# Single-head attention steps, weights split two half tiles ahead, an opening in program order, and a last down product by column halves, in a two-layer hybrid decoder trunk

## The chip, the core and the metric

The kernel runs on one core of a Trainium2 chip. Its five engines run their own instruction streams in order: TensorE (PE, with its weight loads as PEld), VectorE (DVE), ScalarE (ACT), GpSimd (POOL) and SyncE (SP), which issues the large weight transfers. The metric is the device time in microseconds, the median of the runs; one execution is also profiled. Times in the profile count from the start of the profiled span.

## The reference

Two layers over 256 tokens of width 1024, batch 1, all float32:

```python
proj = x @ w_in[l]                        # q, k, v, conv (3 parts), memory queries, three gates
y_attn = diff_attention(rope(q), rope(k), v, lam, ...)     # 8 heads, two score maps per head
y_conv = short_gated_conv(cb, cc, cu, conv_w[l])
y_mem = memory_attention(qm, mem, w_mem_kv[l])             # 4 heads on 256 memory tokens
merged = sum of sigmoid(gate_i) * (y_i @ w_br_i)
x = layer_norm(ALPHA * x + merged @ w_out[l])
f = grouped_moe(x, ...)                   # 16 experts, the two best of one group of four per token
x = layer_norm(ALPHA * x + f)
```

## The kernel before

**Weights.** `plan` lists every weight tile of about 1 MB in the order of its use, and SP's queue fetches them in this order, `ahead` tiles in front of the use, into a ring of 19 buffers of 8 KB per partition (tag "L"). All other large tiles lie in the same ring. Outside the experts, a product in float32 accuracy is made of three fast ones: `pump` splits half a weight tile on ACT (`hl`, the rounded high part, L177) and DVE (the rest, L179), and `ws_block` multiplies high by high, high by low and low by high. The activations are split likewise (`th`/`tl` for the current input, L204 and L205). One *unit* is such a product with one half tile: 24 matmuls of 256 columns in `ws_block` (L215 to L218), or 12 of 512 columns in `mv_units` (L361). `use` hands out the next split half and calls `pump` only when none is ready. Expert weights are used whole and unsplit (`whole`).

**Order.** PE's instructions stand in program order (`manual_schedule`). DVE's and ACT's order is made by a scheduler, save in sections that name those engines too; each engine then runs its list strictly in order.

**Opening.** PE transposes the memory tokens (L290), the keys and values of memory follow (`mem_units`, eight units), then the input `x` is transposed. The tables of the rotary embedding (`sin`, `cos`, 25 small DVE operations and two on ACT) are written behind this in the program.

**Mixers.** `proj` is a generator that yields after every unit: `q` and `k` of a pair of heads (with the rotation on ACT and DVE, L472 to L477), `v`, memory queries, convolution. The loop in `mixers` takes six jobs, four pairs of heads and two pairs of memory heads, and lets `fill` run units between their parts: scores of both heads, 5200, the end of the job before, 5200, both transposes, 2600, the product with `v` (a unit counts 2600). Before the first pair, in layer 0 only, `columns` and `sums` turn small parameters into columns; `sums` has two exponentials (`lexp`) for lambda. Gates and branch products follow for four column blocks, then `w_out`.

**Experts.** `moe` routes the tokens, then runs eight pairs of experts: `project` (gate and up, L1061), `gated`, `hidden` (transposes, L1083), `down` (L1096), `combine` (L1110, into four accumulators). In the last pair the residual is rebuilt on DVE (`xt` from `xl` and `xh`, L1133, then gain and shift `gb`, L1146), the next layer's memory is transposed, and an overflow branch (L1156), not taken here, is passed after the last `down`. Then come `residual` (L314, with row sums), `moments`, `normalise`, and the next layer's `mem_units`.

Of the kernel before, what the change touches and what calls it, by code (L numbers as in the profile page):

```python
# [20 lines left out]
D = 1024  # L21
# [17 lines left out]
WARM = 5  # L39
FILL = 20700  # L40
NU = 5
APART = (5200, 5200, 2600)
# [11 lines left out]
def trunk(ctx: ExitStack, tc: tile.TileContext, x, mem, positions, w_in, lq1, lk1, lq2, lk2, subln, conv_w,  # L54
# [31 lines left out]
    def proj_tiles(w, p):  # L86

        return [([((slice(0, 4),), w[2 * p + i].rearrange("(p k) n -> p k n", p=128)[:, h * 4:h * 4 + 4, :])], (4, 512))
                for h in range(2) for i in range(2)]

    def down_tiles(w, p):
        return [([((slice(0, 2),), w[2 * p + i].rearrange("(p k) n -> p k n", p=128)[:, h * 2:h * 2 + 2, :])], (2, 1024))
                for h in range(2) for i in range(2)]
# [64 lines left out]
    def pump(n=1):  # L158

        while n > 0:  # L160
            if not halves:
                i = state["taken"]
                if i == len(plan):
                    return
# [28 lines left out]
    def use():  # L193
        if not ready:
            pump()
        return ready.pop(0)
# [85 lines left out]

    def transposed(src):
# [20 lines left out]

    def residual(xt, acc, st, t):

        sm = sb.tile([128, 2], F32, name="rsum", bufs=4)
        for c in range(2):
            added(xt, acc, sm, t, c)
        moments(xt, sm, st, t)  # L310
# [56 lines left out]

    mT = {0: transposed(mts.pop(0))}
# [15 lines left out]
    for name, quarter in (("sin", 0.0), ("cos", 0.25)):  # L384
# [20 lines left out]
        rope[name] = tab  # L405
    cosb = rope["cos"][:, None, :].to_broadcast([128, 2, S])
# [50 lines left out]
    def proj(l, xT, qk, vt, br, late2):  # L457
# [9 lines left out]
        for p in range(4):  # L467
# [11 lines left out]
            if p % 2 == 0:  # L479
# [8 lines left out]
        for j in range(2):  # L488
# [17 lines left out]
            split(ych[:, 2 * j:2 * j + 2, :], ycl[:, 2 * j:2 * j + 2, :], y)  # L506

# [12 lines left out]
    def attention(l, p, qk, vt, yT, values):  # L520

        q, k = qk.pop((p, "q")), qk.pop((p, "k"))
        probs = {}
        segs = ((0, 128), (128, 384))
        for h in range(2):
# [23 lines left out]
            nc.vector.tensor_scalar(st[:, 2, 1], st[:, 2, 1], par["nlam"][:, l:l + 1], None, op0=OP.mult)  # L549
# [5 lines left out]
            probs[h] = pr[0]  # L555
        yield
        aT = []
        for h in range(2):
            b = bank([128, 3, 128], "acc")
            for i in range(3):  # L560
                nc.tensor.transpose(b[:, i, :], probs[h][:, i * 128:(i + 1) * 128], ident)
            a = small([128, 3, 128], F32, "aT")
            nc.scalar.activation(a, b, AF.Copy)
            aT.append(a)
        yield
        values(p // 2)
        o = bank([128, 2, 2, 128], "acc")
        for h in range(2):
            c = (2 * p + h) * 128
            a = aT[h]  # L570
            mm(o[:, h, 0, :], a[:, 0, :], vt[:, 0, c:c + 128], start=True, stop=True)
            mm(o[:, h, 1, :], a[:, 1, :], vt[:, 0, c:c + 128], start=True, stop=False)
            mm(o[:, h, 1, :], a[:, 2, :], vt[:, 1, c:c + 128], start=False, stop=True)
        sq = small([128, 128], F32, "sq")
        ss = sb.tile([128, 2, 2], F32, name="ss", bufs=2)
        for h in range(2):
            for qb in range(2):
                nc.scalar.activation(sq, o[:, h, qb, :], AF.Square, scale=128.0 ** -0.5,
                                     accum_out=ss[:, h, qb:qb + 1])
        ss4 = ss.rearrange("p a b -> p (a b)")  # L580
        nc.gpsimd.tensor_scalar(ss4, ss4, EPS, None, op0=OP.add)
        nc.gpsimd.tensor_tensor(ss4, ss4, mhalf, op=OP.pow)
        on = small([128, 2, 2, 128], F32, "on")
        nc.vector.tensor_mul(on, o, ss[:, :, :, None].to_broadcast([128, 2, 2, 128]))
        yield
        b = bank([128, 2, S], "acc")
        for h in range(2):
            for qb in range(2):
                nc.tensor.transpose(b[:, h, qb * 128:(qb + 1) * 128], on[:, h, qb, :], ident)
        split(yT[0][:, 2 * p:2 * p + 2, :], yT[1][:, 2 * p:2 * p + 2, :], b, par["subs"][:, l:l + 1])  # L590

    def mem_attention(km, vm, h0, br, late2):

        qm = br["qm"]
        probs = []
        for h in (h0, h0 + 1):
            b = bank([128, 2, S], "acc")
            for qb in range(2):
                mm(b[:, qb, :], qm[h // 2][:, h % 2, qb * 128:(qb + 1) * 128], km[h // 2][:, h % 2, :], start=True, stop=True)
# [3 lines left out]
            probs.append(pr)  # L603
        yield
        pT = []
        for i in range(2):
            b = bank([128, 2, S], "acc")
            for qb in range(2):
                for m in range(2):
                    nc.tensor.transpose(b[:, m, qb * 128:(qb + 1) * 128],  # L610
                                        probs[i][:, qb, m * 128:(m + 1) * 128], ident)
            a = small([128, 2, S], F32, "pT")
            nc.scalar.activation(a, b, AF.Copy)
            pT.append(a)
        yield
        b = bank([128, 2, S], "acc")
        for i in range(2):
            h = h0 + i
            for m in range(2):
                mm(b[:, i, :], vm[m][:, h * 128:(h + 1) * 128], pT[i][:, m, :], start=(m == 0), stop=(m == 1))  # L620
        late2()
        ymh, yml = br["m"]
        split(ymh[:, h0:h0 + 2, :], yml[:, h0:h0 + 2, :], b)
        yield

    def mixers(l, xT):
# [24 lines left out]
        def values(i):  # L651
            while (i, "v") not in qk:
# [3 lines left out]
        prev = None  # L656
        for p in range(6):
            if not par:
                fill(5000)
                args = columns()  # L660
                fill(5000)
                sums(*args)
            while ((p, "k") not in qk) if p < 4 else ("qm" not in br):
                next(gen)
            if p == 0:
                late()
                fill(2600)
            job = (attention(l, p, qk, vt, yT, values) if p < 4 else
                   mem_attention(km, vm, 2 * (p - 4), br, late2))
            next(job)  # L670
            fill(APART[0])
            if prev:
                next(prev, None)
            fill(APART[1])
            next(job)
            fill(APART[2])
            next(job)
            prev = job
# [38 lines left out]
        for j in range(4):  # L717
            tg = []
            for i in range(3):
# [4 lines left out]
                t = small([128, 2, S], F32, "tg")  # L724
                nc.scalar.activation(t, b, AF.Tanh, scale=0.5)
                tg.append(t)
# [156 lines left out]

    def warm(n):

        if n:
            b = bank([128, 4, 128], "acc")
            for _ in range(n):
                for i in range(4):
                    mm(b[:, i, :], identb, onesb, start=True, stop=True)  # L890

    def moe(l, xt, mix, run, n):
# [195 lines left out]

        def down(h):
# [124 lines left out]
```

## Time and profile before

| | |
|---|---|
| median of 3 runs | 1168.04 us (1167.74 to 1169.44) |
| the profiled execution | 1167.97 us, its span 1166.2 us |
| PE busy | 1071.4 us (92%), 6793 matmul records |
| DVE, ACT busy | 536.6 us (46%), 431.6 us (37%) |
| transfers | 311.77 MB, 267 GB/s over the span |
| mean granted TensorE clock | 0.972 |

The span is made of stages with different limits, so the shares over all of it say little; the rows further down go by stage. A clock of 1.00 is 2.4 GHz; where a stretch shows less, a part of it ran at 1.2 GHz.

### The profile page before, as it was taken

To read this page: it belongs to the slowest core of one execution; us is meant where nothing else is said; L and a number is where in the kernel's file an instruction comes from. 1 tells how busy PE (TensorE), PEld (TensorE's weight loads), DVE (VectorE), ACT (ScalarE), POOL (GpSimd) and SP (SyncE) were. 2 spreads that over 40 slices of the span, in tenths; PEclk is the share of its full clock that TensorE was granted. 3 is DMA by queue.
4 is the path that set the end of the run, shared out by engine and by line. 5 is a ranking of instruction groups with operands and counts; after the bars stand their busy time and mean duration, and the time that the engine had idled before them with its cause. 6 is when DMAs were issued, how large, how long until landed. Compare 5 with 4: busy or idle time off the path is not lost. (4 is left out here: it accounts for less than half of the span.)

```text
span 1166.2 us, 16571 instructions
## 1 busy us (share of the span) xinstructions
PE 1071.4 (92%) x6793; PEld 784.7 (67%) x6793; DVE 536.6 (46%) x914; ACT 431.6 (37%) x752; POOL 42.2 (4%) x95
## 2 busy tenths in 40 slices
PE   4997899999999999999679989999999999999995
PEld 4887899999985334433268878999999843434332
DVE  6667757455553111111466687465456521111116
ACT  3657645444443111110146576444444321111101
POOL 2000000000001000000010000000000010000001
PEclk9999999999998999999889999999999899999998
DMA  9934424556596999999996424345656879999993
GB/s 310 343 113 127 127 76 142 160 186 195 183 377 262 419 422 421 421 420 420 398 292 189 137 83 141 108 145 161 189 193 219 359 299 422 422 420 421 422 418 132
DMA packets 118674, 311.77 MB, mean 267 GB/s; under 512 B 5459, under 2 KB 83505, under 8 KB 94017
## 3 DMA queue, kind: packets, MB, share of 16 engines
q1 hardware_dynamic: 116192, 304.63, 70.2%
q0 software_dynamic: 1824, 5.37, 1.2%
q8 instruction: 55, 0.90, 0.3%
q10 hardware_dynamic: 576, 0.66, 0.2%
q14 instruction: 27, 0.21, 0.0%
HBM read 309.58 MB, written 1.05 MB: 266 GB/s over the span
## 5 line engine op out<-in xcount | busy, mean ns | idle before, releaser
L179 DVE TENSOR_TENSOR hl<-raw,hl 128x1024 fp32r<-128x1024 f32 x192 | 231.1, 1223 | 118.3 <-ACT hl L177 117.9
L215 PE MATMUL ps_g<-th,hl 128*128 128x256 f32 x960 | 244.2, 291 | 20.4 <-ACT hl L177 20.4
L177 ACT ACTIVATE hl<-raw 128x1024 fp32r<-128x1024 f32 x192 | 198.0, 1059 | 126.3 <-PE ps_g L218 60.1
L216 PE MATMUL ps_g<-tl,hl 128*128 128x256 f32 x960 | 240.2, 287 | 0.0
L1061 PE MATMUL ps_g<-raw,xg 128*64 128x512 f32 x1024 | 232.5, 599 | 7.8 <-DVE xg L920 2.8
L215 PEld LDWEIGHTS ps_g<-th,hl 128*128 128x128 f32 x960 | 187.7, 196 | 24.3 <-ACT hl L177 22.0
L216 PEld LDWEIGHTS ps_g<-tl,hl 128*128 128x128 f32 x960 | 188.0, 196 | 0.3
L1061 PEld LDWEIGHTS ps_g<-raw,xg 128*64 128x64 f32 x1024 | 71.9, 137 | 144.8 <-issue 129.1
L218 PE MATMUL ps_g<-th,hl 128*128 128x256 f32 x960 | 136.0, 285 | 0.5 <-DVE hl L179 0.5
L218 PEld LDWEIGHTS ps_g<-th,hl 128*128 128x128 f32 x960 | 125.1, 194 | 0.8 <-DVE hl L179 0.8
L1096 PE MATMUL ps_g<-raw,hT 128*64 128x512 f32 x512 | 114.5, 595 | 0.3 <-DMA raw<-in_w_exp_down 0.3
L205 DVE TENSOR_TENSOR yl<-ps_g,yh 128x512 fp32r<-128x512 f32 x32 | 22.0, 692 | 140.2 <-ACT yh L204 140.2
L1096 PEld LDWEIGHTS ps_g<-raw,hT 128*64 128x64 f32 x512 | 35.5, 137 | 69.5 <-issue 67.6
L1074 DVE SCALAR_TENSOR_TENSOR h<-ps_g,gs,gate 128x512 f32<-128x512 f32 x16 | 18.0, 1123 | 102.5 <-PE ps_g L1061 102.5
L204 ACT ACTIVATE yh<-ps_g 128x512 fp32r<-128x512 f32 x32 | 19.1, 597 | 117.6 <-PE ps_g L1096 117.6
L361 PE MATMUL ps_g<-hl,th 128*128 128x512 f32 x192 | 53.0, 408 | 2.0 <-ACT lexp L442 1.5
L1085 ACT ACTIVATE hT<-ps_g 128x256 f32<-128x256 f32 x16 | 6.1, 383 | 121.7 <-PE ps_g L1083 121.7
L922 ACT ACTIVATE xg<-ps_g,norm 128x256 f32<-128x256 f32 x32 | 17.4, 563 | 78.1 <-PE ps_g L925 78.1
L361 PEld LDWEIGHTS ps_g<-hl,th 128*128 128x128 f32 x192 | 36.1, 195 | 12.2 <-issue 2.0
L925 PE MATMUL ps_g<-pf,xh 128*128 128x256 f32 x128 | 33.3, 323 | 9.5 <-ACT xg L922 7.9
L920 DVE TENSOR_SCALAR xg<-ps_g,norm 128x256 f32<-128x256 f32 x32 | 16.9, 543 | 50.2 <-PE ps_g L925 48.2
L925 PEld LDWEIGHTS ps_g<-pf,xh 128*128 128x128 f32 x128 | 23.8, 206 | 23.6 <-issue 13.1
(239 smaller groups left out, 1306.6 us busy)
## 6 DMA issues: line engine op xcount, KB each, us to landing
raw<-in_w_in SPq DMA_DIRECT2D x64, 1024.0 KB, 5.7
raw<-in_w_exp_gate SPq DMA_DIRECT2D x64, 1024.0 KB, 13.9
raw<-in_w_exp_up SPq DMA_DIRECT2D x64, 1024.0 KB, 15.3
raw<-in_w_exp_down SPq DMA_DIRECT2D x64, 1024.0 KB, 19.0
raw<-in_w_mem_kv SPq DMA_DIRECT2D x8, 1024.0 KB, 13.9
raw<-in_w_br_attn SPq DMA_DIRECT2D x8, 1024.0 KB, 5.1
raw<-in_w_out SPq DMA_DIRECT2D x8, 1024.0 KB, 5.0
raw<-in_w_br_conv SPq DMA_DIRECT2D x8, 512.0 KB, 3.7
```

Source lines behind the costliest of these rows:

```text
L177: nc.scalar.activation(hi, src, AF.Copy)
L179: nc.vector.tensor_tensor(lo, src, hi.bitcast(F32), op=OP.subtract)
L204: return (nc.scalar.activation(hi, src, AF.Copy), nc.vector.tensor_tensor(lo, src, hi.bitcast(F32), op=OP.subtract))
L205: nc.vector.tensor_tensor(lo, src, hi.bitcast(F32), op=OP.subtract))
L215: mm(dst, wh[:, k0 + k, :], ah[:, k, :], start=(k == 0), stop=False)
L216: mm(dst, wh[:, k0 + k, :], al[:, k, :], start=False, stop=False)
L218: mm(dst, wl[:, k0 + k, :], ah[:, k, :], start=False, stop=(k == n - 1))
L361: mm(b[t], a[:, k, t * 128:(t + 1) * 128], ww[:, kk, :], start=(k == 0 and a is ah and ww is wh), stop=(k == KD - 1 and ww is wl))
L925: mm(b, (xl if low else xh)[:, t, k * 128:(k + 1) * 128], PF[g][:, t], start=first, stop=last)
L1061: mm(b[both[i]], xg[:, k, c + i * CAP:c + (i + 1) * CAP], w[i][:, kk, :], start=(k == 0), stop=(k == KD - 1))
L1074: nc.vector.scalar_tensor_tensor(h.rearrange("q f p -> q p f"), u.rearrange("q (p f) -> q p f", f=4), GS[p // 2][:, p % 2:p % 2 + 1], g.re ...
L1096: mm(bs[c][both[i]], h[:, 2 * j + f, both[i]], w[i][:, f, c * 512:(c + 1) * 512], start=(j == 0 and f == 0), stop=(j == 1 and f == 1))
```

## The change

The edits, without new names for what stays:

- **Opening.** DVE and ACT follow program order there too, and 56 small matmuls (`warm(WARM0)`) stand in PE's order ahead of the first transposes.
- **Weights.** `use` keeps two split halves in reserve (`LEAD`); `pump` stops at expert tiles (marked by a third field) and at tiles not fetched.
- **Mixers.** `v` follows the odd pairs instead of the even ones. Pairs become objects with `score`, `turn`, `mix` and `done`; twelve steps take one head each, with the end of older jobs at a step's start and the transposes of the previous head inside the step. Three units lie in each step. The three gate blocks of the first column block move from behind the loop into the generator.
- **Experts.** In the third last pair, `ahead` falls to 12, and `xt` and the gains are allocated and fetched (they were in the last but one); gain and shift are applied in the last but one pair. The overflow branch stands ahead of the last down product. This product takes all four tiles and makes one column half after the other (`down_last`); the first half is combined and added to the residual in the middle of the second. Between layers, `pump(4)` splits four halves of the next weights before the last combination.

```diff
-APART = (5200, 5200, 2600)
+APART = (5200, 2600)
+LEAD = 2
+WARM0 = 14
...
     def use():
-        if not ready:
-            pump()
+        pump(max(0, LEAD + 1 - len(ready)))
         return ready.pop(0)
...
+    opening = ExitStack()
+    opening.enter_context(tc.manual_schedule(engines={mybir.EngineType.DVE, mybir.EngineType.Activation}))
+    warm(WARM0)
     mT = {0: transposed(mts.pop(0))}
...
         rope[name] = tab
+    opening.close()
...
-            if p % 2 == 0:
+            if p % 2:
                 c = (p // 2) * 512
                 yield from mv_units(xT, [vt[:, t, c:c + 512] for t in range(2)])
...
-        for p in range(6):
-            if not par:
-                fill(5000)
-                args = columns()
-                fill(5000)
-                sums(*args)
-            while ((p, "k") not in qk) if p < 4 else ("qm" not in br):
-                next(gen)
...
+        if not par:
+            fill(7800)
+            args = columns()
+            fill(7800)
+            sums(*args)
+        until((1, "q"), qk)
+        late()
+        jobs, n = {}, 12
+        for i in range(n + 2):
+            if i % 2 and i > 2:
+                j = (i - 3) // 2
+                if j < 4:
+                    until((j // 2, "v"), qk)
+                jobs[j].mix()
+            elif i > 3:
+                jobs[(i - 4) // 2].done()
+            if i < n:
...
+                jobs[j].score(i % 2)
             fill(APART[0])
+            if 0 < i <= n:
+                jobs[(i - 1) // 2].turn((i - 1) % 2)
             fill(APART[1])
...
+        def down_last(h, mid):
+            w = [(whole(), whole()) for _ in range(2)]
+            ys = []
+            for c in range(2):
+                b = bank([128, 512])
+                for j in range(2):
+                    if c and j:
+                        mid(ys[0])
+                    for f in range(2):
+                        for i in range(2):
+                            mm(b[both[i]], h[:, 2 * j + f, both[i]], w[j][i][:, f, c * 512:(c + 1) * 512],
+                               start=(j == 0 and f == 0), stop=(j == 1 and f == 1))
...
+            if p == last - 2:
+                state["ahead"] = 12
+                xt = big([128, 2, D], F32, "xt")
+                gb = gain_shift(ln1_g[l], ln1_b[l])
...
+        ys = down_last(hT[0], half)
+        if l + 1 < DEPTH:
+            pump(4)
+        combine(last, ys, (1,))
```

How this moves instructions, at three places. The first is ACT's list in the opening of layer 0. `th` are the split transposed activations, `hl` the split weights, `kv` the keys of memory, `sw` the swapped halves for the rotation, `sin` and `cos` its tables, `lexp` the exponentials of `sums`. Before, it begins:

```order
L404 ACT_TABLE_LOAD
L404 ACTIVATE sin<-r,cc 128x256
L402 ACTIVATE cos<-r 128x256
L204 ACTIVATE th<-ps_g 128x512 x4
L177 ACTIVATE hl<-raw 128x1024 x6
L346 ACTIVATE kv<-ps_g 128x512 x2
```

Now it begins:

```order
L206 ACT_TABLE_LOAD
L206 ACTIVATE th<-ps_g 128x512 x4
L179 ACTIVATE hl<-raw 128x1024 x4
L349 ACTIVATE kv<-ps_g 128x512
L179 ACTIVATE hl<-raw 128x1024 x2
```

and has further on, around the first exponentials:

```order
L479 ACTIVATE sw<-ps_g 32x512
L480 ACTIVATE sw<-ps_g 32x512
L179 ACTIVATE hl<-raw 128x1024 x2
L479 ACTIVATE sw<-ps_g 32x512
L449 ACT_TABLE_LOAD
L449 ACTIVATE lexp<-ps_g 128x2
L408 ACT_TABLE_LOAD
L408 ACTIVATE cos<-r 128x256
L449 ACT_TABLE_LOAD
L449 ACTIVATE lexp<-ps_g 128x2
```

The two tables no longer stand ahead of the first split; `cos` now stands between the two exponentials, with a table load at each turn.

The second place is DVE's list in the attention of layer 0, where the third pair's keys are rotated (`k<-k,sw` is the last step of it) and the scores of its first head are masked (the first step after the score matmuls). `on` is the normalised output of the pair before. Before:

```order
L476 TENSOR_TENSOR sw<-sw,sin 128x512
L207 SCALAR_TENSOR_TENSOR yl<-ps_acc,subs,yh 128x512
L477 TENSOR_TENSOR q<-q,sw 128x512
L179 TENSOR_TENSOR hl<-raw,hl 128x1024 x2
L475 TENSOR_TENSOR k<-ps_g,cos 128x512
L476 TENSOR_TENSOR sw<-sw,sin 128x512
L179 TENSOR_TENSOR hl<-raw,hl 128x1024
L477 TENSOR_TENSOR k<-k,sw 128x512
L179 TENSOR_TENSOR hl<-raw,hl 128x1024 x3
L536 TENSOR_TENSOR ps_acc<-ps_acc,cmask 128x2x128 x2
L538 TENSOR_REDUCE sm<-ps_acc 128x1 x4
L584 TENSOR_TENSOR on<-ps_acc,ss 128x512
```

Now:

```order
L484 TENSOR_TENSOR k<-k,sw 128x512
L570 RECIPROCAL sm<-sm 128x4
L571 TENSOR_SCALAR sm<-sm,nlam 128x2
L574 TENSOR_SCALAR p<-p,sm 128x128
L574 TENSOR_SCALAR p<-p,sm 128x256
L575 SCALAR_TENSOR_TENSOR p<-p,sm 128x128
L575 SCALAR_TENSOR_TENSOR p<-p,sm 128x256
L482 TENSOR_TENSOR q<-ps_g,cos 128x512
L483 TENSOR_TENSOR sw<-sw,sin 128x512
L484 TENSOR_TENSOR q<-q,sw 128x512
L209 SCALAR_TENSOR_TENSOR yl<-ps_g,subs,yh 128x512
L558 TENSOR_TENSOR ps_acc<-ps_acc,cmask 128x2x128 x2
```

Between a pair's keys and its first mask there now lie the rest of a head of the pair before and the next pair's queries; `on` no longer stands behind the first mask of the next pair.

The third place is DVE's list at the end of the experts of layer 0: `yl` are split down products, `h` the gated hidden rows, `tl` the next layer's split memory, `hT` half of the transposed `h` that the last down product needs. Before:

```order
L205 TENSOR_TENSOR yl<-ps_g,yh 128x512 x2
L1074 SCALAR_TENSOR_TENSOR h<-ps_g,gs,gate 128x128x4
L1133 TENSOR_TENSOR xt<-xl,xh 128x1024 x2
L1146 TENSOR_TENSOR xt<-xt,gb 128x1024 x4
L205 TENSOR_TENSOR tl<-ps_g,th 128x512 x4
L1086 COPY hT<-ps_g 128x256
```

Now:

```order
L207 TENSOR_TENSOR yl<-ps_g,yh 128x512 x2
L1178 TENSOR_TENSOR xt<-xl,xh 128x1024 x2
L1194 TENSOR_TENSOR xt<-xt,gb 128x1024 x4
L1098 SCALAR_TENSOR_TENSOR h<-ps_g,gs,gate 128x128x4
L207 TENSOR_TENSOR tl<-ps_g,th 128x512 x4
L1110 COPY hT<-ps_g 128x256
```

The six operations on `xt` stood between `h` and `tl` and now stand ahead of `h`.

## Rows read from the trace of the kernel before

**Rows 1.** Busy time of the engines by stage, with the granted clock (PEclk), the share of the transfer engines and GB/s: the mixers of layer 0 in two stretches, gates and branches, routing, experts, the step between the layers, and the same of layer 1.

```profile
60.00:105.00 45.00, 41.68 (x301) 38.02 (x302) 30.04 (x78) 27.74 (x72) 1.31 (x2) 1.00 0.39 117
105.00:180.00 75.00, 67.81 (x492) 63.14 (x491) 49.85 (x103) 42.18 (x106) 4.11 (x6) 0.93 0.36 113
180.00:330.00 150.00, 147.80 (x1159) 144.96 (x1157) 86.96 (x96) 70.65 (x86) 0.00 (x0) 0.99 0.56 180
365.00:570.00 205.00, 194.47 (x944) 77.11 (x940) 33.78 (x55) 28.47 (x52) 4.09 (x12) 1.00 1.00 416
570.00:600.00 30.00, 17.39 (x69) 10.39 (x70) 18.71 (x28) 9.40 (x13) 4.59 (x6) 0.73 0.92 317
600.00:690.00 90.00, 83.31 (x586) 75.95 (x586) 63.10 (x111) 57.96 (x114) 1.29 (x2) 1.00 0.57 173
690.00:780.00 90.00, 82.62 (x614) 78.92 (x615) 58.37 (x118) 47.60 (x112) 4.16 (x6) 0.94 0.37 115
```

**Rows 2.** What PE waited for in the mixers of layer 0 (60 to 330 us): the waiting line, the releasing one, us in total, times, longest.

```profile
PE ps_acc L531 <- DVE on L584: 4.4, 1, 4.4
PE ps_acc L531 <- DVE k L477: 4.4, 2, 2.8
PE ps_g L215 <- ACT hl L177: 2.2, 1, 2.2
PE ps_g L361 <- ACT lexp L442: 1.5, 1, 1.5
```

**Rows 3.** The same in the mixers of layer 1 (600 to 780 us).

```profile
PE ps_acc L531 <- DVE k L477: 5.1, 3, 2.8
PE ps_g L215 <- ACT hl L177: 4.3, 2, 2.2
```

**Rows 4.** Instructions of the opening in order of time (start, us, instruction, idle time before it and its releaser), and the landing times of the two weight transfers issued from 1.6 to 2.1 us (shortest, median, longest).

```profile
8.51 3.46 PE L290 MATMUL ps_g<-ident,mt 128*128 128x128 f32 x15 [1.74 <-DMA mt<-in_mem]
...
16.75 0.42 ACT L402 ACTIVATE cos<-r 128x256 f32<-128x256 f32 x1 [1.27 <-DVE r L399]
17.07 2.04 ACT L204 ACTIVATE th<-ps_g 128x512 fp32r<-128x512 f32 x4
18.98 5.81 ACT L177 ACTIVATE hl<-raw 128x1024 fp32r<-128x1024 f32 x6
20.11 0.58 PE L215 MATMUL ps_g<-th,hl 128*128 128x256 f32 x1 [8.13 <-ACT hl L177]
24.52 0.28 PE L215 MATMUL ps_g<-th,hl 128*128 128x256 f32 x1
27.40 0.28 PE L215 MATMUL ps_g<-th,hl 128*128 128x256 f32 x1
...
DMA to landing us min/median/max: 10.0/11.2/12.5
```

**Rows 5.** Instructions around `columns` and `sums` in layer 0, in order of time.

```profile
55.11 0.37 DVE L428 TENSOR_REDUCE wbs<-wr 128x16 f32<-128x128 f32 x1
56.78 0.69 DVE L475 TENSOR_TENSOR q<-ps_g,cos 128x512 f32<-128x512 f32 x1
59.11 0.70 DVE L477 TENSOR_TENSOR q<-q,sw 128x512 f32<-128x512 f32 x1
...
59.91 1.28 ACT L442 ACT_TABLE_LOAD   x1
61.20 0.23 ACT L442 ACTIVATE lexp<-ps_g 128x2 f32<-128x2 f32 x2
61.55 0.59 ACT L473 ACTIVATE sw<-ps_g 32x512 f32<-32x512 f32 x1
```

**Rows 6.** PE around the score matmuls of the third pair of layer 0.

```profile
111.44 1.14 PE L531 MATMUL ps_acc<-k,q 64*128 64x128 f32 x10
117.01 1.65 PE L531 MATMUL ps_acc<-k,q 64*128 64x128 f32 x6 [4.43 <-DVE on L584]
118.59 2.07 PE L361 MATMUL ps_g<-hl,th 128*128 128x512 f32 x4
...
124.10 1.07 PE L361 MATMUL ps_g<-hl,tl 128*128 128x512 f32 x4
```

**Rows 7.** Instructions from the last up product of layer 0 to the first product of layer 1, in order of time.

```profile
561.68 3.65 PE L1061 MATMUL ps_g<-raw,xg 128*64 128x512 f32 x14 [1.32 <-DMA raw<-in_w_exp_up]
576.14 1.12 PE L1083 MATMUL ps_g<-ident,h 128*128 128x128 f32 x4 [8.93 <-DVE tl L205]
580.24 7.09 PE L1096 MATMUL ps_g<-raw,hT 128*64 128x512 f32 x32
595.55 0.58 PE L215 MATMUL ps_g<-th,hl 128*128 128x256 f32 x1 [5.80 <-ACT hl L177]
...
566.34 4.61 DVE L1133 TENSOR_TENSOR xt<-xl,xh 128x1024 f32<-128x1024 f32 x2
570.73 4.75 DVE L1146 TENSOR_TENSOR xt<-xt,gb 128x1024 f32<-128x1024 f32 x4
```

**Rows 8.** The end of layer 1, in order of time.

```profile
1151.25 0.60 ACT L204 ACTIVATE yh<-ps_g 128x512 fp32r<-128x512 f32 x1 [1.06 <-PE ps_g L1096]
1152.93 0.50 PE L1110 MATMUL ps_acc<-yl,ct 128*128 128x512 f32 x1 [1.09 <-DVE yl L205]
1156.43 1.15 ACT L320 ACTIVATE sqx<-xt,lnst 128x1024 bf16<-128x1024 f32 x1 [4.58 <-DVE lnst L318]
```

More of the change, by code (lines that the diff above doesn't have):

```diff
@@ L280, in trunk, with warm @@
     cmask2 = cmask[:, None, :].to_broadcast([128, 2, 128])
+    def warm(n):
+        if n:
+            b = bank([128, 4, 128], "acc")
+            for _ in range(n):
+                for i in range(4):
+                    mm(b[:, i, :], identb, onesb, start=True, stop=True)
     def transposed(src):
@@ L506, in proj, with gate @@
             split(ych[:, 2 * j:2 * j + 2, :], ycl[:, 2 * j:2 * j + 2, :], y)
+        tg = br["tg"] = []
+        for _ in range(3):
+            b = yield from one()
+            tg.append(gate(b))
+    def gate(b):
+        t = small([128, 2, S], F32, "tg")
+        nc.scalar.activation(t, b, AF.Tanh, scale=0.5)
+        return t
     def softmax_parts(b, width, scale, n=2):
@@ L563, in attention @@
             nc.scalar.activation(a, b, AF.Copy)
[L564 to L573, printed above, removed]
@@ L717, in mixers @@
         for j in range(4):
-            tg = []
-            for i in range(3):
+            tg = br["tg"] if j == 0 else []
+            while len(tg) < 3:
                 b = bank([128, 2, S])
@@ L723, in mixers @@
                     ws_block(b[:, h, :], w[h], xT)
[L724 to L726 removed]
+                tg.append(gate(b))
             if 0 < j < 3:
@@ L1087, in hidden @@
             return hT
+        def down_last(h, mid):
[7 more added lines that the diff above has]
+                    for f in range(2):
+                        for i in range(2):
+                            mm(b[both[i]], h[:, 2 * j + f, both[i]], w[j][i][:, f, c * 512:(c + 1) * 512],
+                               start=(j == 0 and f == 0), stop=(j == 1 and f == 1))
+                yh, yl = small([128, 512], F32R, "yh"), small([128, 512], F32R, "yl")
+                split(yh, yl, b)
+                ys.append((yh, yl))
+            return ys
         def down(h):
@@ L1143, in moe @@
                 hT.append(hidden(h))
+            if pend is not None:
+                combine(*pend)
+            steps(4)
+            if p == last - 1:
                 for t in range(2):
@@ L1146, in moe, with half @@
                         nc.vector.tensor_tensor(xt[:, t, :], xt[:, t, :], gb[:, i, :], op=op)
-            if pend is not None:
-                combine(*pend)
-            steps(4)
-            pend = p, down(hT[0])
-            steps(4)
             if p < last:
+                pend = p, down(hT[0])
+                steps(4)
                 u = project(p + 1)
-            else:
-                most = nc.values_load(cnti[0:1, 0:1], min_val=0, max_val=S)
-                with tc.If(most > CAP):
-                    overflow(l, xt, gx)
-        for c in range(2):
-            combine(*pend, (c,))
-        return xt, acc
+        most = nc.values_load(cnti[0:1, 0:1], min_val=0, max_val=S)
+        with tc.If(most > CAP):
+            overflow(l, xt, gx)
+        sums = [sb.tile([128, 2], F32, name="rsum", bufs=4) for _ in range(2)]
+        def half(y):
+            combine(last, [y], (0,))
+            for t in range(2):
+                added(xt, acc[t], sums[t], t, 0)
+        ys = down_last(hT[0], half)
+        if l + 1 < DEPTH:
+            pump(4)
+        combine(last, ys, (1,))
+        return xt, acc, sums
     for l in range(DEPTH):
-        xt, acc = moe(l, xt, *mixers(l, xT))
+        xt, acc, sums = moe(l, xt, *mixers(l, xT))
         last = l + 1 == DEPTH
```

164 lines of the change are left out of this document (78 added, 86 removed).

## The prediction

> **What bounds the kernel now.** I read the busy time by stage first. In the experts the transfer engines are full (share 1.00, 416 GB/s) while PE is nearly always busy too [rows 1]; that stage ends by the transfers and the change leaves its order alone. In the gates and branches PE is busy 147.80 of 150 us [rows 1]. The idle time of PE lies elsewhere, and there the next view, who waited for whom, names it: the opening (8.13 us for the first split weight [rows 4]), the mixers (PE idle 45.00 - 41.68 + 75.00 - 67.81 + 150.00 - 147.80 = 12.7 us in layer 0, and 6.69 + 7.38 = 14.1 us in layer 1 [rows 1]), and the step between the layers (8.93 and 5.80 us [rows 7]). DVE and ACT are idle a third of the mixers [rows 1], so these waits are of order and distance, not of an engine that is full. Each long wait is also paid a second time: after the 4.43 us wait the 16 matmuls from 118.59 to 124.10 took 5.5 us, against about 4 by the pace of the four that follow [rows 6], and the granted clock of those stretches is 0.93 and 0.94 [rows 1]. The same holds at the start: the first unit took 24.52 - 20.11 = 4.4 us, the second 27.40 - 24.52 = 2.9 [rows 4]. So a removed stall of some 4 us or more is worth about 1.5 us beyond its length.
>
> **The change part by part.** The sum is made against the profiled execution's own 1167.97 us (span 1166.2, so 1.8 lie around it), which is 0.07 below the median of the runs. Negative is a gain.
>
> *Start of the opening.* ACT now splits the transposed memory at once instead of after `sin` and `cos`, which ended about 17.1 [rows 4]. What is late next: the first weights land at about 1.65 + 10.0 = 11.7 us, the sixteen transposes end at 11.97 [rows 4]. Then the last of four `th` splits (2.04 / 4 = 0.5) and half a weight tile (5.81 / 6 = about 1.0) have to pass ACT: 11.97 + 0.5 + 1.0 = 13.5; if the warm-up matmuls make the transposes quicker, the landing sets it: 11.7 + 1.0 = 12.7. I take 13.2 against 20.11, so -6.9 (bounds -6.6 and -7.4). The 56 small matmuls end before the tokens land at 8.51 or push the first transposes by a little; they lie in PE's idle time. If the clock is up when the first unit begins, 1.5 more is gained [rows 4]; I take half, -0.7.
>
> *Constants.* Here a rival of the gain has been built into the order. `cos` now stands on ACT between the two `lexp`, and `lexp` needs a matmul that PE reaches only after six units. From the end of these units PE then waits for: one `sw` copy 0.59, table load 1.28, `lexp` 0.2, table load 1.28, `cos` 0.42, on DVE `q` times `cos` 0.69, the sum 0.70, four reductions of 0.37 less their overlap with each other and two small products between them, together about 1.8: 7.0 us, where 1.5 was waited before [rows 2, 4, 5]. Cover there is none, since the next unit stands behind this matmul in PE's list. Above 4 us it also costs the slow stretch, 1.7. So +5.5 and +1.7. The bounds: 1.5 as before if DVE and ACT find time to run ahead, and 7.0 plus two weight splits of DVE (1.2 each) put between these operations, 9.4. I stay at 7.0, since every member of the chain stands in the lists in this order. The Trainium skill speaks against this order: its page "ScalarE: Activation LUTs", section "Rules for kernel authors", asks to group functions by table set, and the section "What ACT_TABLE_LOAD costs" puts a change of set at about 2.66 us, load and drain. Here the load took 1.28 us and the next function began at 61.20, right at its end, so this trace shows no drain [rows 5]; by the page the two changes ahead of `cos` would make the wait some 2.8 us longer and the sum 1121 instead of 1118. Start and constants together: -6.9 - 0.7 + 5.5 + 1.7 = -0.4.
>
> *Attention, layer 0.* The waits after the constants are for the rotated keys 4.4, for `on` 4.4 and for split weights 2.2 [rows 2]. Keys: before, one unit (2.9 us) lay between the end of a `k` product and the scores that need it, while four `sw` copies (2.4 us) and three DVE operations (2.1 us) must pass and DVE's list had weight splits between them; now at least three units lie there (8.7 us) for all pairs behind the first. `on` stood behind the next pair's first mask on DVE, while PE's second scores waited for the bank that `on` empties: a ring of waits that a step without a second head ahead of it doesn't have. Split weights are now two halves (5.8 us) ahead. So 11.0 of waits go, and the slow stretches: the clock lacks 0.07 x 75 + 0.01 x 150 = 6.8 us, of which about 1.5 fell into idle time, so 5.3 [rows 1]. What is late next is the step's `mix`: it stands one unit (2.9 us) behind the last `turn`, and the copy of the transposed head must pass ACT in that time. The same distance stood there before and no wait for it is in the list [rows 2]. The new load: the same work of DVE (30.04 + 49.85 us in 120) in some 105 us is 76% [rows 1], denser than before. I leave 2 us of waits: -16.3 + 2 = -14.3.
>
> *Attention, layer 1.* PE idle 14.1 us [rows 1], most of it for keys 5.1, split weights 4.3 and, in one wait as long as in layer 0, `on` [rows 3]; clock 0.06 x 90 = 5.4, less 0.9 in idle time. No constants here. -18.6 + 2 = -16.6.
>
> *Moved `v`, gate blocks, objects.* The units are the same; the six gate units fill steps instead of standing behind them. No instruction is added. The two further split halves take two of the ring's 19 buffers from the transfers, which were 0.36 to 0.57 busy in the mixers [rows 1]: hidden; if that cover were gone, each late tile would cost up to its 2.5 us (1.05 MB at 416 GB/s).
>
> *Between the layers.* PE ended the transposes at 567.2 (565.25 and 1.97 for sixteen, from the end of the up product at 561.68 + 3.65 = 565.3) and began `hidden` at 576.14, since `tl`, which empties its bank, stood on DVE behind `xt` (4.61 and 4.75 us) [rows 7]. Now these 9.4 us run ahead of `h`, under the up product, and end near 565.9. Then `h` 1.1, the first `tl` 0.7: `hidden` starts at 567.7. Half a microsecond for it, eight combining matmuls 1.9, the branch 0.2, the down product 7.1 with 1.0 of combination inside: 578.4. The second half's split takes 0.6 on ACT and 0.7 on DVE, with the signals 1.4, then 1.0: 580.8. `pump(4)` lets the next unit start there, against 595.55: -14.7; and its slow first unit (1.5) goes too, since no wait longer than 1.4 is left, -1.5 and 0.5 for a wait behind it. -16.7. Transfers nearly bind: the last up tiles landed at 561.7 [rows 7], the four down tiles follow at 2.5 us each, 564.2 to 571.7, and the third is needed at 572.2, since `down_last` takes all four in its first half. The margin is 0.5 us. The memory weights follow until 581.7, the first at 574.2. The smaller `ahead` and the earlier gains (1 MB in the same full stage) add no bytes.
>
> *End.* DVE is no longer at `xt` when the last split comes, and half the additions are done: combination and `sqx` come about 1.1 us earlier than 1156.43 [rows 8]. -1.1.
>
> Sum: -0.4 - 14.3 - 16.6 - 16.7 - 1.1 = -49.1, and 1167.97 - 49.1 = 1118.9; **1118** with the median's scatter.
>
> **The rivals.** (a) *The attention stays bound by DVE and ACT.* The denser steps use up the distance; half of the waits and of the slow stretches stay: half of 16.3 + 18.6 is 17, less the 4 already left: 1132. For it: 76% load in lists run in order. Against it: a third of both engines' time was free. (b) *No new wait at the constants and none left in the attention*: 1118 - 7 - 4 = 1107. Against it stands ACT's list. (c) *Transfers take over between the layers*: `down_last` waits for its third and fourth tile, with the gains in the way; one or two tiles of 2.5 us in each layer, 1123 to 1128. (d) *Slower than before*: the copy of a transposed head waits on ACT behind the next head's four exponentials, and `mix` or the next scores behind it on PE. There are 24 steps; from 49 / 24 = 2.0 us in each on, the change loses. With 3 us, 1118 + 72 = 1190. The rows show no such wait at the same distance. (e) *The order does not change what is waited for* and all stays within 0.2%: the lists say otherwise at every place.
>
> **How the numbers follow.** My forecast holds with 0.64 (its own range 1111 to 1126), (a) 0.15, (b) 0.09, (c) 0.06, (d) 0.04, (e) 0.02. A range from 1107 to 1134 takes in the first, most of (a) and (b), and (c). Faster by over 0.2% (2.3 us, about what the scatter of the runs lets one tell): 0.64 + 0.15 + 0.09 + 0.06 = 0.94; same 0.02, slower 0.04.
>
> **What would show it.** The first unit near 13 us; a PE wait of 6 to 8 us for `lexp` and `wbs` near 57; no waits for `k`, `on` or split weights over 1 us afterwards, and a clock of 0.98 or more in both mixers; the first product of layer 1 some 15 us sooner after the last up product; the experts as long as before. Wrong would be: waits of 1 to 3 us in front of `turn`, `mix` or the scores in most steps, a down product broken by transfers, or experts that start later than the mixers gained.

## The result, and the profile after

The changed kernel takes 1129.86 us in the median (1128.89 to 1130.87) beside 1168.34 us for the kernel before in the same comparison: a ratio of 0.967, with a 95% interval of 0.9653 to 0.9686. That is 38.5 us less, inside the range that was forecast and 12 us above the value. The profiled execution took 1130.69 us, its span is 1128.9 us.

The difference of the two spans, 37.3 us, cut at instructions that both traces have (columns: span of the stretch before and after, in us):

| stretch | before | after | change | forecast |
|---|---|---|---|---|
| start to first unit | 20.11 | 12.65 | -7.5 | -6.9 |
| to the first `w_out` product of layer 0 | 233.41 | 225.73 | -7.7 | -0.7 + 5.5 + 1.7 - 14.3 = -7.8 |
| to the end of the last up product of layer 0 | 311.81 | 310.87 | -0.9 | 0 |
| to the first memory unit of layer 1 | 30.22 | 15.63 | -14.6 | -14.7 |
| to the first mixer unit of layer 1 | 29.07 | 33.46 | **+4.4** | -2.0 |
| to the first expert product of layer 1 | 311.46 | 296.90 | -14.6 | -16.6 |
| to the end of its last up product | 204.36 | 202.79 | -1.6 | 0 |
| to the end of the span | 25.76 | 30.87 | **+5.1** | -1.1 |

Two rows miss by 6 us each, the memory units of layer 1 and the end; all others are within 2 us. The mixers, busy time by stage as in [rows 1] (the stretch and its length; busy us and instructions of PE, PE's weight loads, DVE, ACT and GpSimd; granted clock; share of the transfer engines; GB/s):

```profile
60.00:105.00 45.00, 40.28 (x267) 36.17 (x268) 32.13 (x77) 29.18 (x66) 0.53 (x2) 0.89 0.39 120
105.00:180.00 75.00, 74.53 (x572) 70.06 (x571) 57.68 (x119) 48.09 (x118) 4.99 (x7) 1.00 0.41 127
180.00:330.00 150.00, 150.00 (x1161) 145.88 (x1160) 83.36 (x102) 65.72 (x81) 0.93 (x3) 1.00 0.62 207
600.00:690.00 90.00, 89.01 (x651) 81.08 (x650) 73.57 (x144) 67.78 (x140) 2.55 (x4) 1.00 0.52 164
690.00:780.00 90.00, 90.00 (x731) 88.71 (x730) 56.56 (x95) 46.51 (x93) 2.95 (x4) 1.00 0.45 142
```

From 105 us on PE is never idle for more than a microsecond in the mixers and its clock stands at 1.00, although DVE works 73.57 of 90 us. What is left of waits is elsewhere. PE's longest single ones, over the whole span (us in total, times, longest):

```profile
PE ps_g L364 <- DVE hl L181: 5.5, 1, 5.5
PE ps_g L455 <- DVE wbs L435: 4.3, 1, 4.3
PE ps_g L1124 <- PEq L1200: 4.1, 2, 3.7
...
PE ps_g L448 <- ACT lexp L449: 2.5, 1, 2.5
PE ps_g L217 <- ACT hl L179: 2.4, 1, 2.4
```

The second and fourth are the stall at the constants that was forecast. The first and third were not. The first, in order of time on three engines (GpSimd, DVE, PE):

```profile
569.14 0.36 POOL L324 TENSOR_SCALAR lnst<-lnst 128x1 f32<-128x1 f32 x1 [68.78 <-ACT sqx L323]
569.79 0.58 POOL L307 DMA_DIRECT2D gb<-in_ln_g  x1 [0.28 <-issue]
...
577.86 2.48 DVE L328 SCALAR_TENSOR_TENSOR xt<-xt,lnst,gb 128x1024 f32<-128x1024 f32 x2 [7.15 <-DMA gb<-in_ln_g]
...
582.65 6.89 DVE L181 TENSOR_TENSOR hl<-raw,hl 128x1024 fp32r<-128x1024 f32 x6
...
583.93 3.78 PE L364 MATMUL ps_g<-hl,th 128*128 128x512 f32 x8 [5.50 <-DVE hl L181]
```

Gain and shift of the second norm (`gb`) are fetched by GpSimd, and this fetch now stands behind a step of the norm (`lnst`) that waits for row sums. Before, it was issued at 571.24 us, 20.9 us before its use at 592.12; now at 569.79, when DVE is about to ask for it (577.86 - 7.15 = 570.7). DVE waits 7.15 us, six weight splits queue behind, and PE stands 5.5 us. The lists of GpSimd show it, before and now:

```
L297 DMA gb<-in_ln_g 128x1024
L298 DMA gb<-in_ln_b 128x1024
L321 TENSOR_SCALAR lnst<-lnst 128x1
L322 TENSOR_TENSOR lnst<-lnst,mhalf 128x1
```

```
L324 TENSOR_SCALAR lnst<-lnst 128x1
L307 DMA gb<-in_ln_g 128x1024
L308 DMA gb<-in_ln_b 128x1024
L325 TENSOR_TENSOR lnst<-lnst,mhalf 128x1
```

The third wait is the overflow branch, at the end of layer 1. PE in order of time, and then PE's branch instructions, each by itself, first the two of the kernel now and then the two of the kernel before (shortest, median and longest ns, first and last start):

```profile
1101.39 0.39 PE L1152 MATMUL ps_acc<-yl,ct 128*128 128x512 f32 x1
1105.46 7.07 PE L1124 MATMUL ps_g<-raw,hT 128*64 128x512 f32 x24 [3.68 <-PEq L1200]
```

```profile
L1200 PEldq COMPARE_BRANCH  x1: 353/353/353, 552.0 to 552.0; - x1
L1200 PEldq COMPARE_BRANCH  x1: 5252/5252/5252, 1099.8 to 1099.8; - x1
```

```profile
L1156 PEldq COMPARE_BRANCH  x1: 3175/3175/3175, 583.5 to 583.5; - x1
L1156 PEldq COMPARE_BRANCH  x1: 345/345/345, 1147.2 to 1147.2; - x1
```

The branch that isn't taken costs PE's sequencer 0.35 us in layer 0 and 5.25 us in layer 1. Before, it was the other way round: 3.2 us in layer 0, at 583.5 us and so under the last down product (580.24 to 587.33 [rows 7]), and 0.35 us in layer 1. Now the long one falls in layer 1, and four transposes and eight combining matmuls, 2.5 us, lie in front of the wait. Behind the wait the 24 matmuls take 7.07 us (granted clock 0.79 from 1105 to 1113 us), as long as 32 did before.

### The profile page after: what moved, and what is told of

The parts are those of the page before. It is cut to its first block, busy times and chain, and to the rows that moved or that the text cites. A ratio compares the mean times of both kernels' runs of the same rounds, so it can differ in the third digit from the quotient of the medians.

```text
span 1128.9 us, 16660 instructions
## 1 busy us (share of the span) xinstructions
PE 1068.5 (95%) x6849; PEld 781.7 (69%) x6849; DVE 534.6 (47%) x914; ACT 436.4 (39%) x755; POOL 40.5 (4%) x95
## 3 DMA queue, kind: packets, MB, share of 16 engines
q0 software_dynamic: 1824, 5.37, 1.2%
## 5 line engine op out<-in xcount | busy, mean ns | idle before, releaser
L218 PEld LDWEIGHTS ps_g<-tl,hl 128*128 128x128 f32 x960 | 185.7, 193 | 0.4
L1138 PE MATMUL ps_g<-raw,hT 128*64 128x512 f32 x448 | 100.1, 595 | 0.0
L1138 PEld LDWEIGHTS ps_g<-raw,hT 128*64 128x64 f32 x448 | 31.1, 137 | 60.0 <-issue 58.5
L364 PEld LDWEIGHTS ps_g<-hl,th 128*128 128x128 f32 x192 | 36.6, 196 | 14.4 <-DVE hl L181 5.9
L949 PEld LDWEIGHTS ps_g<-pf,xh 128*128 128x128 f32 x128 | 23.7, 206 | 23.6 <-issue 13.1
## 6 DMA issues: line engine op xcount, KB each, us to landing
raw<-in_w_mem_kv SPq DMA_DIRECT2D x8, 1024.0 KB, 12.6
```

Source lines behind the costliest of these rows:

```text
L218: mm(dst, wh[:, k0 + k, :], al[:, k, :], start=False, stop=False)
L364: mm(b[t], a[:, k, t * 128:(t + 1) * 128], ww[:, kk, :], start=(k == 0 and a is ah and ww is wh), stop=(k == KD - 1 and ww is wl))
L949: mm(b, (xl if low else xh)[:, t, k * 128:(k + 1) * 128], PF[g][:, t], start=first, stop=last)
L1138: mm(bs[c][both[i]], h[:, 2 * j + f, both[i]], w[i][:, f, c * 512:(c + 1) * 512], start=(j == 0 and f == 0), stop=(j == 1 and f == 1))
```

## The experiments

The runs come from several chips, each measured beside the kernel before on the same chip, so ratios are compared: the changed kernel has 0.967, and 0.001 is 1.17 us. Every ratio carries about 0.0015 either way, so differences under 2.5 us are read from the traces, not from the times.

**The step between the layers.** `gb_early` moves the fetch ahead of the branch, `gb_mid` only ahead of the four splits:

```diff
+        gb2 = gain_shift(ln2_g[l], ln2_b[l])        # gb_early: here
         most = nc.values_load(cnti[0:1, 0:1], min_val=0, max_val=S)
...
         ys = down_last(hT[0], half)
+        gb2 = gain_shift(ln2_g[l], ln2_b[l])        # gb_mid: here
         if l + 1 < DEPTH:
             pump(4)
```

> The changed kernel, with gain and shift of the second norm fetched ahead of the overflow branch instead of behind it, so that they no longer stand behind a waiting step of that norm on GpSimd. Theory (the late gain and shift hold DVE's list for 7.2 us between the layers, the weight splits queue behind them, and PE pays 5.5 us and then some 2.4 us at the slow clock): DVE's wait for them and PE's wait for a split weight in the memory units go, and the time falls by 6 to 8 us from 1129.9, to about 1123. Rival (the lost time lies in the attention, whose steps are bound by DVE and ACT): PE's wait reappears elsewhere and the time stays within 1 us of 1129.9. A third outcome, 2 to 4 us: the splits are late for DVE's own work even without the wait.

> The changed kernel with gain and shift of the second norm fetched between the last down product and the split of four weights: later than in the run that fetched them ahead of the branch, where the last down product then waited 1.6 us for a tile, but still ahead of the waiting norm steps on GpSimd. Theory: no wait for a down tile and none for gain and shift over 1 us: the first unit of layer 1 some 2.5 us sooner than in that run, so 9 to 11 us below the changed kernel. Rival (the buffer they go into is free only at the end of the down product, so that they come late again): DVE waits 2 to 7 us for them, and the run falls between the two.

`gb_early` has 0.9601 (0.9588 to 0.9614), 8 us less; `gb_mid` 0.9595 (0.9582 to 0.9609), 8.8 us less. In both DVE's wait for `gb` is gone, and from the first memory unit of layer 1 to its first mixer unit 24.75 us pass instead of 33.46. So the late fetch and what follows from it cost 8.7 us: 5.5 of wait, the rest at a slow clock (mean 0.85 from 577 to 600 us, 1.00 in `gb_early`). PE's waits between the layers, in `gb_early` and in `gb_mid`:

```profile
PE ps_g L1124 <- DMA raw<-in_w_exp_down: 1.6, 1, 1.6
```

```profile
PE ps_acc L1152 <- ACT yh L206: 0.7, 1, 0.7
```

The earlier fetch makes the last down product wait 1.6 us for a tile, as rival (c) had it, and the first memory unit comes 2.6 us later; the later fetch gives 1.6 us of that back, less than the 2.5 that were expected. (It is issued at 546.28 us, ahead of the last down product at 551.99, so its buffer was free by then and the rival of that expectation falls.)

**The branch.** `no_branch_l1` leaves it out in layer 1, `no_branch` in both layers, `branch_early` puts it one product sooner:

```diff
                 pend = p, down(hT[0])
+                if p == last - 1:
+                    most = nc.values_load(cnti[0:1, 0:1], min_val=0, max_val=S)
+                    with tc.If(most > CAP):
+                        overflow(l, xt, gx)
                 steps(4)
                 u = project(p + 1)
```

> The changed kernel without the overflow branch of layer 1 (left out: a branch that this input does not take). Theory (the branch ahead of the last down product costs PE's sequencer a jump that nothing covers, 3.7 us, and then 1.7 us of slow matmuls): the down product follows the combination at once, 5 to 5.5 us less, about 1124.5. Rival (PE waits there for something else that the trace puts down to the branch, as the down tiles): the wait stays, under 1 us is gained.

> The changed kernel without the overflow branch in both layers (left out: branches that this input does not take). Beyond the run with one branch less: 0.4 us for PE's wait in layer 0 if the memory transposes cover the jump there, as the trace says; and up to 2 us if the wait of SyncE at the branch holds back the first weights of layer 1. So 1122 to 1124.5.

> The changed kernel with the overflow branch behind the down product of the last but one pair, where PE has 32 matmuls of 0.22 us queued. Theory (a jump costs PE nothing where some 5 us of queued matmuls cover it): the wait of 3.7 us in layer 1 falls below 0.5 and about as much is gained as without the branch, 4 to 5 us. Rival (SyncE's wait at the branch, now earlier, holds back weight transfers, and the experts wait for them): PE waits over 3 us for tiles behind the branch, and nothing is gained.

`no_branch_l1`: 0.9631 (0.9618 to 0.9644), 4.6 us less; the down product follows the end of the up product after 3.7 us, not 7.4, and the rest of the span is 0.9 us shorter. The theory holds, with less behind the wait than the 1.7 us put down, because the next limit is near: the weight loads of this down product now wait for its last tiles:

```profile
1105.16 0.20 PEld L1124 LDWEIGHTS ps_g<-raw,hT 128*64 128x64 f32 x4 [0.66 <-DMA raw<-in_w_exp_down]
```

`no_branch`: 0.9553 (0.954 to 0.9566), 13.7 us less, far more than expected. The trace tells why: without the branch in layer 0 the fetch of `gb` is ordered ahead of `lnst` again, DVE waits 1.0 us for it, and the stretch of the memory units takes 24.7 us. The gain is that of `gb_mid` and that of `no_branch_l1` in one (8.8 + 4.6 = 13.4): what the branch of layer 0 cost was the place of the fetch, not time of PE.

`branch_early`: 0.9768 (0.9755 to 0.9782), 11.4 us **slower**. On PE the branch now takes 0.33 and 0.35 us and nothing waits for it. But:

```profile
PE ps_g L1085 <- DVEq L1199: 21.2, 2, 10.6
```

```profile
542.74 4.63 DVE L1194 TENSOR_TENSOR xt<-xt,gb 128x1024 f32<-128x1024 f32 x4
```

The up product, whose bank DVE had emptied by 538.5 us, begins at 547.68, where DVE has passed the branch behind its six operations on the residual. Behind a branch PE waited for all that DVE had in front of it.

**The constants.** `sums_late` puts `sums` behind the queries of the second pair, `tables_early` runs the operations of the rotary tables as a generator, six behind each of the first five memory units. `no_opening` takes the program order of DVE and ACT and the small matmuls away:

```diff
-    opening.enter_context(tc.manual_schedule(engines={mybir.EngineType.DVE, mybir.EngineType.Activation}))
-    warm(WARM0)
```

> The changed kernel with the exponentials and the router sums of the constants placed behind the queries of the second pair, so that sine and cosine stand together on ACT and the two exponentials behind them. Theory (PE waits 2.5 and 4.3 us for the exponentials and the sums, and then runs slow for 1.7 us): both waits shrink below 1 us together and the time falls by 6 to 8 us, to about 1123. Rival (the opening is bound by the work of ACT and DVE, so that the same wait moves to the first rotated keys or to a split weight): less than 2 us.

> The changed kernel with the 25 small DVE operations and the two ACT functions of the rotary tables written between the first five memory units instead of behind the opening. The run with later sums gave 3 us and left PE waiting 3.8 us for rotated queries and keys: so the order on ACT was only one half of the stall. Theory (the other half is the work for the tables, 25 operations or 8.6 us, that DVE does at 46 to 60 us among splits and rotations): put where DVE waits anyway, it goes, and with it both waits of 2.5 and 4.3 us and the slow stretch: 6 to 8 us less than the changed kernel's ratio of 0.967, so 0.960 to 0.962. Rival (the opening has no free time on DVE, and the tables then delay the split of x): a wait of some 4 us for the split x near 30 us, and under 3 us gained.

> The changed kernel with DVE and ACT free to be reordered in the opening and without the 56 small matmuls. Theory (the opening in program order gains 6.9 to 7.5 us at the first unit and loses 6.8 us of waits and 1.7 us of slow matmuls at the constants, since the tables then stand among the exponentials): the first unit is late again, near 20 us, the waits for the exponentials and the router sums shrink to 1.5, and the time is within 2 us of the changed kernel. Rival (the waits at the constants come from elsewhere): they stay, and the time rises by 6 to 8 us.

`sums_late` 0.9627 (0.9614 to 0.964), `tables_early` 0.9639 (0.9626 to 0.9652), 5.0 and 3.6 us less, where 6 to 8 were expected of each. From the transposes of `x` to the first `w_out` product, 209.87 us in the changed kernel, they take 207.09 and 206.26, about half of the expected gain. The wait has moved as the rival of each had it. PE's waits in `sums_late` and in `tables_early`:

```profile
PE ps_g L448 <- DVE k L482: 2.4, 1, 2.4
PE ps_g L448 <- DVE q L482: 1.4, 1, 1.4
```

```profile
PE ps_g L300 <- DVE tl L207: 4.2, 1, 4.2
PE ps_g L217 <- ACT lexp L469: 1.5, 1, 1.5
```

So DVE has no room for the tables' 8.6 us at one place: in front of the rotations they delay these, among the first splits they delay the split of `x`. `no_opening` has 0.9686 (0.9667 to 0.9704), 1.9 us more: the first unit is at 19.70 us, the stall at the constants has shrunk to its 1.5, and the same stretch takes 203.2 us. The opening gained 7 us and its tables cost 6.7, as the theory had it. Two other stretches of this run changed by about as much, against each other: the way from the last up product to the next layer takes 5.2 us more than in the changed kernel (20.82), the end 4.6 less (26.2). PE's stall near the branch now lies in layer 0 and not in layer 1, with no edit there:

```profile
559.49 6.67 PE L1122 MATMUL ps_g<-raw,hT 128*64 128x512 f32 x24 [4.20 <-issue]
```

**The attention.** `lead0` sets `LEAD = 0` in the changed kernel; `before_lead2` gives the kernel before the reserve alone:

```diff
-        if not ready:
-            pump()
+        pump(max(0, LEAD + 1 - len(ready)))
```

> The changed kernel with no split half in reserve (each is split when it is asked for, as before). Theory (the reserve of two is what removed the waits for split weights, 2.2 us in layer 0 and 4.3 in layer 1, with slow matmuls behind them): such waits come back and the time rises by 4 to 10 us, ratio 0.971 to 0.976 against 0.967. Rival (the single-head steps alone keep DVE and ACT in time): under 2 us.

> The kernel before with nothing but the reserve of two split halves (and the marks that stop the splitting at expert tiles). Theory (waits for keys and for the normalised output come from the order of the pairs, 4.4 and 4.4 us in layer 0, 5.1 and 4.4 in layer 1, and only the waits for split weights from the missing reserve): 4 to 8 us less than before, waits for keys and output stay. Rival (with a reserve PE survives all of them, since DVE and ACT are free for the attention when it comes): 20 us or more, as much as the whole attention part of the change.

`lead0`: 0.9734 (0.9715 to 0.9753), 7.5 us more, as much as expected, but at other places. Its trace is 3.8 us late at the transposes of `x` and loses 2.3 us in the mixers of layer 0 and 2.8 in the memory units of layer 1. In the mixers of layer 1 (first unit to the first `w_out` product) it takes 189.07 us against 188.66. There the reserve does nothing: the single-head steps alone keep the splits in time. `before_lead2`: 0.9898 (0.988 to 0.9916), 11.9 us less than before and more than the 4 to 8 expected: 5.1 from the transposes of `x` to the first `w_out` product, 3.7 in the same stretch of layer 1 (199.53 against 203.23), the rest in smaller pieces outside. PE's wait for `on` in the mixers of layer 1 before (the keys are in [rows 3]), and then its waits there in `before_lead2`:

```profile
PE ps_acc L531 <- DVE on L584: 4.4, 1, 4.4
```

```profile
PE ps_acc L531 <- DVE k L477: 4.6, 2, 3.0
PE ps_acc L531 <- DVE on L584: 4.0, 1, 4.0
```

The waits for keys and for `on` stay, those for splits go. So the waits for keys and output belong to the order of the pairs, and those for splits go by either part of the change; the steps give 14.2 of layer 1's 14.6 us by themselves.

**The three repairs together.** `all_three` joins `tables_early`, `gb_mid` and `branch_early`. `all_three_b` spreads the tables thinner and puts the branch behind the up product of the last pair instead:

> The changed kernel with the three edits of this call together: early tables, gain and shift between down product and splits, early branch. If the three costs are independent of each other, the gains add up: 6 to 8, 9 to 11 and 4 to 5 us, 19 to 24 in all, a time of about 1108 us. If they share a cause, or if the experts' transfers take back what comes sooner, it is under 15 us.

> The changed kernel with tables spread over the opening (three of their operations behind each of the first five memory units, four behind each later one), gain and shift of the second norm fetched ahead of the splits between the layers, and the overflow branch behind the up product of the last pair, so that no work of DVE but that on the residual lies ahead of it. In the trace of the changed kernel PE's own branch instruction takes 5.25 us in layer 1 and 0.35 in layer 0; 3.6 us of queued matmuls and 1.3 us of waiting for the gated rows now lie behind it. Theory (three independent late waits): 5 to 7 us, 8.7 us and about 3.5 us less, together 17 to 19, ratio 0.951 to 0.953. Rival for the branch (DVE's pass again holds PE, as in the run with the branch one product sooner): a wait of PE for DVE's branch of some us in both layers, ratio above 0.956.

`all_three`: 0.9679 (0.9665 to 0.9692), no better than the changed kernel: the waits at the branch, 10.6 us in each layer, eat the rest. `all_three_b`: 0.957 (0.955 to 0.9591), 1118.52 us in the median, 11.7 us less than the changed kernel and the fastest here that leaves nothing out, though less than expected. The tables and `gb` gave what they should (the stretch to `w_out` 204.6 us, that of the memory units 24.75). The branch gave about 1 us: the end is 2.2 us shorter than in the changed kernel (28.7), but the way from the last up product to the next layer is 1.1 longer than in `gb_mid` (17.78 against 16.66). In layer 0 the transposes wait for DVE's branch, as the rival had it, and in layer 1 PE stands behind its own, now 0.35 us short, without a releaser:

```profile
PE ps_g L300 <- DVEq L1224: 1.9, 1, 1.9
```

```profile
PE ps_g L1130 <- issue: 3.0, 1, 3.0
```

## Why the prediction came out as it did

**Right, by its steps.** The start: 12.65 us against 13.2. The constants: waits of 2.5 + 4.3 = 6.8 against 7.0, then slow matmuls (clock 0.68 from 56 to 70 us); `no_opening` shows the whole as 6.7, forecast 7.2 (its 1.7 for the slow stretch stands in no row; [rows 6] give 1.5). The attention: 14.4 us in layer 0 (217.61 against `no_opening`'s 203.2), forecast 14.3, and 14.6 in layer 1, forecast 16.6. The way from the last up product to the next layer: 14.6, forecast 14.7, and step by step too: from the end of the up product `hidden` begins after 2.1 us (2.4), the last down product ends after 13.4 (13.1), and the first unit begins after 15.6 (15.5). In the layer step no down product waits for a tile. No run takes the edits of this step apart, so what each of them is worth is read from one trace and not shown; the same holds for the moved `v` and gate blocks. On the table loads ahead of the exponentials and of `cos` the trace again agrees with the row: each took 1.28 us and the next function began right at its end. It doesn't show the load and drain of about 2.66 us that the Trainium skill's page "ScalarE: Activation LUTs", section "What ACT_TABLE_LOAD costs", puts on a change of set.

**Wrong, in two terms.** First, "since no wait longer than 1.4 is left": between the layers a wait of 5.5 us was left, and the term came out at +4.4 instead of -2.0. The step had followed `tl`, `h` and the splits on DVE, and the transfers on SyncE, but not GpSimd's list, where the fetch of `gb` changed places with a step of the norm; `gb_mid` gives the 8.7 us back. Second, the end: its term counts the earlier additions and puts the branch at nothing, though the change moves the branch of layer 1, too, from behind the last down product to ahead of it. "The branch 0.2" stands in the layer step alone, and there PE waited 0.41. In the kernel before the long branch, 3.2 us, was out of sight under a down product of 7.09 us; PE's wait behind the branch of layer 1 was 0.16. The change took the cover away in both layers, and the long branch, now 5.25 us and in layer 1, showed: `no_branch_l1` measures 4.6 us. That the long one now falls in layer 1, no row of before could tell. Without the branch the end would still have come out at +0.4 instead of -1.1 (from the last up product's end to the end of the span 26.2 us against 25.8): there the first 24 matmuls of the down product take 6.21 us, against 5.37 in layer 0, as they wait for tiles; the other 0.7 stays open. The two misses are 12.6 us; the other six rows of the table together are 0.8 us better than forecast.

**The rivals.** The time lies near that of (a), 1132, but (a) is refuted: the dense steps leave no wait over 1.0 us. (b) falls by the constants. (c) did not happen, yet `gb_early` shows how near it was. (d) is out: the waits for a transposed head sum to 1.4 us. (e) is out by the time. The forecast's own range, 1111 to 1126, was missed by 4 us. The wider range held by luck: it was stretched for cases that did not happen, and what filled it, the late fetch and the bare branch, none of them names.

## What to carry to other kernels

Price a moved instruction by the longest of its own rows, not by the wait seen behind it: the wait is what its cover left over, and the row of one layer does not stand for the next. Follow every queue past which a step moves, that of a nearly idle engine too: a small fetch that changed places with one waiting step cost 8.7 us where the whole change gained 38. And look for a place for a branch where no engine has work in front that others need behind it; of the places tried here none was free.

## What the runs showed of the hardware

**A branch on PE cost 0.33 to 0.47 us or 3.2 to 5.25.** The long form shows once in eight of the thirteen kernels with a branch: in layer 0 in the two with the order of before (3.2 and 3.3 us), in layer 1 in six with the changed order (4.8 to 5.25 us). In each of the eight a transfer of the instruction queue q8 falls into the time of the branch; in none of the seventeen short ones. The branch ends 2.5 to 2.6 us after this transfer starts in all eight; the two lengths differ by how late it starts, 0.6 to 0.8 us into the branch in the first two and 2.3 to 2.7 in the other six. Why it starts late is open: weights were in flight in both groups (356 GB/s during the branch of the kernel before, 407 in the changed kernel from 1099.8 us to the start of the transfer). The changed kernel from 1099.8 to 1105.0 us (packets, MB, share of the transfer engines):

```profile
q8 instruction: 1, 0.02, 1.4%
```

In `no_opening` the branches take 0.35 and 0.33 us, but in layer 0 PE then stands 4.2 us without a releaser, and in `all_three_b` 3.0 us in layer 1; both times PE goes on 2.4 to 2.6 us after the start of an instruction transfer. The Trainium skill's page "Runtime: NRT & Kernel Launch", section "Instruction fetch mechanics", says that a taken branch to code outside the loaded pages has to fetch its page by a transfer before it goes on. The transfers at the long branches agree with that; whether PE jumps past the body of a branch that isn't taken, and which page was loaded when, no run here shows.

**With the small matmuls ahead of the first unit, the clock there was full in some executions only.** In the eleven profiles of kernels that have them, the granted clock from 12 to 17.2 us is 1.00 in five and 0.67 in six, though PE's instructions up to there are the same; the transposes of `x` then begin at 26.7 to 27.0 us or at 28.5 to 28.6 (32.3 without the reserve). The changed kernel and `gb_mid` (busy us and matmuls of PE, clock, share of the transfer engines, GB/s):

```profile
12.00:17.20 5.20, 4.55 (x25) 0.67 1.06 333
```

```profile
12.00:17.20 5.20, 4.78 (x40) 1.00 1.05 333
```

The forecast's half of 1.5 us was a mean of two outcomes, and no single execution showed it.
